# Hymba layer: first loads and norms reordered, P's diagonal blocks split between VectorE and ScalarE, another entry into the MLP

## The chip, the cores and the metric

The kernel runs on one core of one Trainium2 chip. The metric is the device time of one execution in microseconds (us). The engines are named as in the profile: PE (TensorE, matmuls and transposes), DVE (VectorE), ACT (ScalarE), POOL (GpSimd) and SP (SyncE, which here only starts DMAs). L12 is line 12 of the kernel's file.

## What is computed

One layer of a hybrid decoder in fp32: 1024 tokens of width 1024 with 16 meta tokens ahead of them (dropped at the end). One input projection feeds two token mixers, a retention with 4 heads and a sparse attention with 8 heads over the 256 best keys of each query; their outputs go through one output projection, and a squared-ReLU MLP of width 4096 follows.

```python
u = rmsnorm(h, norm1_w); proj = u @ w_in
rq, rk, rv, rg, dq, dk, dv, iq, ik, iw = split(proj)
y_ret = retention(rq, rk, rv, rg, ret_norm_w, pos)
# sparse attention, by blocks of 128 queries
score = einsum('bch,bchs->bcs', iw, relu(einsum('bchd,bsd->bchs', iq, ik)))
_, sel = top_k(where(causal, score, NEG), 256)
logits = q @ k[sel] + rel_bias[t5_bucket(dist)]
y_dsa = softmax(where(valid, logits, NEG)) @ v[sel]
h = h + concat([y_ret, y_dsa]) @ w_out
u = rmsnorm(h, norm2_w)
h = h + square(relu(u @ w_ff1)) @ w_ff2
```

## The kernel before, in words

**Products.** Every fp32 matrix is split into a rounded half `hi` and a rest `lo`; a product is three matmuls (hi·hi, hi·lo, lo·hi) into one PSUM bank. The hi half is an ACT copy, the lo half a subtraction on DVE or POOL. PSUM has two rings of banks, `psA` and `psB`.

**Order.** The program is written as Python generators that are woven together (`spread`), and a scheduler then places the instructions of each engine by its own estimate of their readiness, so the order on an engine isn't the order of the text. Each engine runs its own list in order. SP starts nearly all DMAs, in its list's order.

**First stage (0 to about 190 us).** For each block `b` of 128 tokens `do_norm1` (L250) loads `xt` (`load_x`, L177), and `norm_T` (L145) squares it on ACT with the row sum (L149), takes the inverse root on POOL (`rsqrt`, rs_y, L141 and L142), multiplies by it and by the norm's weight row `nrow` on DVE (L151, tile `u`), transposes `u` on PE (L156, eight 128x128) and splits the result (uh, ul). `small_proj` makes the index keys from `u` (weights `wrs`, halves `wsh`/`wsl`, L327 and L328), `index_q` and `index` the index scores (weights of the columns IQ: raws `wr`, L214; halves `wh`/`wl`, L189 and L194). The relative bias is looked up by one matmul with a one-hot table (`hot`, `relt`, L371 to L382): its result `gt` goes to DRAM as `g1`, and is spread there to 128 rows as `gd` (1.47 MB), from which `bias` is read at L438.

**Top-k, retention and attention (about 100 to 600 us).** DVE and ACT find the 256th best score of each query; PE meanwhile does the retention and the projections. Attention runs over eight blocks `i` and two head groups `g`: `attend_p` (L568) makes the logits and their exponentials P, `attend_v` (L607) transposes P on PE (L628), splits it into `ph` halves (ACT L633, DVE L634) and multiplies with the values (L635, L636). The first 16 keys (the meta tokens) of four heads go together: one transpose (L616), a copy `phm` on ACT (L618), and four DVE operations of 32 partitions each (L621) that put the hi rows (`odd` 0) and lo rows (`odd` 1) of each head into its own diagonal block of `pm`; a matmul with `pm` (L638) ends the group. There are 16 groups.

**Output projection and second norm (about 597 to 680 us).** `out_mm` (L689) makes the second half of the columns, block by block; the second half of `w_out` is loaded and split by `out_w(1, True)` when the first of nine pieces is done. `norm2` (L876) of each block follows: Square and row sum on ACT (L879), inverse root on POOL, product `un` on DVE (L881), eight transposes (L889). From these come the operands of the MLP's first layer, a Strassen-like scheme with seven products m = 2, 4, 3, 5, 6, 7, 1, each with its own sums of token halves: U2 and U4 from the blocks 0 to 3; U3, U5, U6 and U7 from the blocks 4 to 7 together with the kept copies `f1` of the first; U1 likewise in the MLP's loop (L1172, L1173). The lo halves (L895) of U4, U3 and U6 are made by POOL, the others by DVE.

**MLP (about 667 us to the end).** 16 column groups `p` with seven products each, one `unit` of 12 matmuls for each product (L1002 to L1004). The units' order is `groups`: products 2 and 4 of p = 1, all of p = 0, the rest of p = 1, then p = 2 and on, so four units need only U2 and U4. `EVAC` says how each product is added into four accumulators (1a, 1b, 2a, 2b): an ACT copy (L1009) where it is the first, a DVE addition (L1012) where not. The second layer follows (`stage2`, L1101, matmuls L1120 to L1122).

Of the kernel before, what the change touches and what calls it, by code (L numbers as in the profile page):

```python
# [81 lines left out]
def layer(ctx, tc, x, meta, norm1_w, w_in, ret_w, q_w, k_w, rel, w_out, norm2_w, w1, w2,  # L82
# [94 lines left out]
    def load_x(b):  # L177
        xt = xin.get(b)
        if xt is None:
            xt = row("xt")  # L180
        nc.sync.dma_start(xt[:, :D], x[128 * b:128 * b + 128, :])
        return xt
# [67 lines left out]
    def do_norm1(b):  # L250
        if b == 8:
            xm = row("xt")
            nc.sync.dma_start(xm[:NM, :D], meta)
            norm_T(xm[:NM, :D], NM, lambda g: (um[:, 4 * g:4 * g + 4, :NM], um[:, 4 * g:4 * g + 4, ML:]))
        else:
            o = 128 * (b % 4)
            xt = load_x(b)
# [111 lines left out]
    L = hot_d.shape[1]
    hot = wp.tile([32, L], F32, tag="rl", name="hot", bufs=2)  # L370
    nc.sync.dma_start(hot, hot_d)  # L371
    relt = const.tile([32, 8], F32, name="relt")
    nc.sync.dma_start(relt, rel)
    g1 = dr.tile([8, L], F32, name="g1")
    gd = dr.tile([128, 8, L], F32, name="gd")
    ps = psA()
    nc.tensor.matmul(ps[:8, :L], relt, hot, start=True, stop=True)
    gt = wp.tile([8, L], F32, tag="rl", name="gt", bufs=2)
    nc.scalar.activation(gt, ps[:8, :L], AF.Copy)
    nc.sync.dma_start(g1, gt)  # L380
    g1a = g1[:]
    nc.sync.dma_start(gd, bass.AP(tensor=g1a.tensor, offset=g1a.offset, ap=[[0, 128], [L, 8], [1, L]]))  # L382
# [839 lines left out]
```

## Time and profile before

| | us |
|---|---|
| median of three runs | 1297.18 |
| the three runs | 1294.48, 1297.18, 1297.89 |
| the profiled execution | 1296.34 |
| its span in the trace | 1294.6 |
| PE busy | 1240.1 (96%) |
| DVE busy | 1022.2 (79%) |
| ACT busy | 757.9 (59%) |
| POOL busy | 221.1 (17%) |

Of the profiled execution 1.7 us lie outside the span. All times in the text are of this one execution, from the span's start. Busy times are shares of the whole span; how an engine stands in one stage is read from the views of a stretch. A matmul's duration in the trace overlaps the next one's, so what a matmul costs PE is read from the distance of two starts.

### The profile page before, as it was taken

The numbers are of one execution on the slowest core, as the hardware profiler recorded it, in microseconds if no ns is written. First come the engines' busy times: TensorE is split into PE (matmuls) and PEld (weight loads), VectorE is DVE, ScalarE is ACT, GpSimd is POOL, SyncE is SP. The second block draws the span as 40 slices with busy tenths as digits, with TensorE's granted clock in tenths as the row PEclk, the third lists the DMA queues.
The fourth block names the chain that finished last, engine by engine and source line by source line (L and its number), as shares of the span: only waits on it lengthen the run. The fifth ranks groups of instructions, "written<-read, shape, count | busy, mean of one in ns | idle before, by whom it ended". The sixth has DMA issues, their size and how long they took to land.

```text
span 1294.6 us, 18365 instructions
## 1 busy us (share of the span) xinstructions
PE 1240.1 (96%) x6032; PEld 1025.8 (79%) x6032; DVE 1022.2 (79%) x2298; ACT 757.9 (59%) x1612; POOL 221.1 (17%) x278
## 2 busy tenths in 40 slices
PE   5999989999999899999898999999999999999998
PEld 4888868887887667877776888888888888888887
DVE  5579999993478899876489777777788887887875
ACT  6567567889956677665356555454565444444442
POOL 4003262424425322101241000000000200000000
PEclk8999999999999999999998999999999999999999
DMA  8103031202113223114953444344539835344222
GB/s 282 60 17 93 25 114 40 73 9 74 58 33 97 91 84 105 69 63 145 321 189 116 149 173 145 130 153 151 176 134 355 341 114 187 122 163 166 91 94 98
DMA packets 101279, 165.06 MB, mean 128 GB/s; under 512 B 8712, under 2 KB 48944, under 8 KB 97472
## 3 DMA queue, kind: packets, MB, share of 16 engines
q1 hardware_dynamic: 101184, 163.90, 36.7%
q8 instruction: 47, 0.77, 0.2%
q14 instruction: 48, 0.39, 0.1%
HBM read 113.46 MB, written 51.85 MB: 128 GB/s over the span
## 4 chain that ended last, share of the span: by engine, by line
PE 69%; DVE 19%; ACT 5%; issue 4%; DMA 2%; POOL 1%; SPq 0%; DVEq 0%; ACTq 0%
PE psB L1120 5%; PE psB L1121 5%; PE psB L1122 5%; PE psB L1002 4%; PE psB L1003 4%; PE psB L1004 4%; PE psA L1003 4%; PE psA L1002 4%; PE psA L1004 4%; DVE jk_cnt L746 3%; PE psA L246 3%; PE psA L247 3%; PE psA L248 3%; PE psA L1120 3%; PE psA L1121 3%
## 5 line engine op out<-in xcount | busy, mean ns | idle before, releaser
L973 ACT ACTIVATE wh<-ga 128x512 fp32r<-128x512 f32 x144 | 87.2, 628 | 159.2 <-PE psB L1121 138.3
L246 PE MATMUL psA<-wh,uh 128*128 128x512 f32 x376 | 150.3, 400 | 1.3 <-DVE fg L488 1.3
L247 PE MATMUL psA<-wh,ul 128*128 128x512 f32 x376 | 149.3, 397 | 0.0
L248 PE MATMUL psA<-wl,uh 128*128 128x512 f32 x376 | 149.1, 397 | 0.0
L974 DVE TENSOR_TENSOR wl<-ga,wh 128x512 fp32r<-128x512 f32 x144 | 96.6, 687 | 47.8 <-ACT wh L973 47.2
L973 ACT ACTIVATE wh<-sum 128x512 fp32r<-128x512 f32 x128 | 78.7, 625 | 79.2 <-DVE sum L970 70.9
L1121 PE MATMUL psB<-wh,wl 128*128 128x512 f32 x280 | 108.9, 389 | 0.0
L1122 PE MATMUL psB<-wl,wh 128*128 128x512 f32 x280 | 108.9, 389 | 0.0
L751 ACT ACTIVATE jk_top<-sc,tcand 128x784 bf16<-128x784 f32 (+2 forms) x93 | 98.3, 1057 | 14.9 <-DVE tcand L821 12.5
L1120 PE MATMUL psB<-wh 128*128 128x512 f32 x280 | 106.8, 389 | 0.0
L974 DVE TENSOR_TENSOR wl<-sum,wh 128x512 fp32r<-128x512 f32 x128 | 88.5, 693 | 4.0 <-ACT wh L973 4.0
L246 PEld LDWEIGHTS psA<-wh,uh 128*128 128x128 f32 x376 | 70.8, 188 | 14.0 <-issue 1.1
L248 PEld LDWEIGHTS psA<-wl,uh 128*128 128x128 f32 x376 | 70.8, 188 | 13.3
L247 PEld LDWEIGHTS psA<-wh,ul 128*128 128x128 f32 x376 | 71.1, 189 | 12.2
L1040 POOL COPY ga<-wl 128x1 f32<-128x1 f32 x8 | 6.6, 828 | 402.6 <-DVE wl L974 359.2
L746 DVE TENSOR_SCALAR_CACHE_REDUCE jk_cnt<-sc,tcand 128x400 bf16<-128x400 f32 (+2 forms) x93 | 70.4, 757 | 1.0
L359 ACT ACTIVATE rl<-psB,absw 128x320 f32<-128x320 f32 (+5 forms) x104 | 52.9, 555 | 28.0 <-DVE sc L363 13.9
L1121 PE MATMUL psA<-wh,wl 128*128 128x512 f32 x168 | 65.4, 389 | 0.0
L1122 PE MATMUL psA<-wl,wh 128*128 128x512 f32 x168 | 65.4, 389 | 0.0
L1120 PE MATMUL psA<-wh 128*128 128x512 f32 x168 | 64.9, 389 | 0.0
L194 POOL TENSOR_TENSOR wl<-wr,wh 128x512 fp32r<-128x512 f32 x44 | 60.3, 1390 | 19.2 <-ACT wh L189 13.9
L633 ACT ACTIVATE ph<-psB 128x512 fp32r<-128x512 f32 x72 | 41.4, 594 | 34.9 <-PE psB L628 26.8
(391 smaller groups left out, 3559.0 us busy)
## 6 DMA issues: line engine op xcount, KB each, us to landing
ga<-hid SPq DMA_DIRECT2D x28, 1024.0 KB, 5.2
wr<-in_w_ff_dram SPq DMA_DIRECT2D x34, 512.0 KB, 5.1
hid<-hs SPq DMA_DIRECT2D x48, 256.0 KB, 2.1
wr<-in_w_in_dram SPq DMA_DIRECT2D x32, 256.0 KB, 3.2
ysd<-ys SPq DMA_DIRECT2D x32, 256.0 KB, 2.8
ys<-ysd SPq DMA_DIRECT2D x32, 256.0 KB, 5.0
gb<-in_w_ff_dram SPq DMA_DIRECT2D x8, 1024.0 KB, 6.8
ga<-in_w_ff_dram SPq DMA_DIRECT2D x8, 1024.0 KB, 5.2
```

The costliest lines, as they stand in the source:

```text
L246: nc.tensor.matmul(ps[:P, :n], uh, wh, start=d == 0, stop=False)
L247: nc.tensor.matmul(ps[:P, :n], ul, wh, start=False, stop=False)
L248: nc.tensor.matmul(ps[:P, :n], uh, wl, start=False, stop=d == 7)
L746: nc.vector.tensor_scalar(jk_[:, :ncol[i]], sc[i], cand[:, j:j + 1], 0.0, op0=ALU.is_ge, op1=ALU.add, accum_out=cnt[:, j:j + 1])
L973: nc.scalar.activation(view(hi), s, AF.Copy)
L974: nc.vector.tensor_tensor(view(lo), s, view(hi).bitcast(F32), op=SUB)
L1002: nc.tensor.matmul(ps, hi[:, a], uh[:, d], start=d == 0, stop=False)
L1003: nc.tensor.matmul(ps, lo[:, a], uh[:, d], start=False, stop=False)
L1004: nc.tensor.matmul(ps, hi[:, a], ul[:, d], start=False, stop=d == 3)
L1120: nc.tensor.matmul(ps[tb], ah[:, t], bh, start=j == 0 and m not in CONT, stop=False, skip_group_check=True)
L1121: nc.tensor.matmul(ps[tb], al[:, t], bh, start=False, stop=False, skip_group_check=True)
L1122: nc.tensor.matmul(ps[tb], ah[:, t], bl, start=False, stop=j == NO - 1, skip_group_check=True)
```

## The change

It has three parts.

**First stage.** The load of block 0 is SP's first DMA, ahead of `ident` and `nrow`. `norm_T` scales `xt` in place (ACT's Square writes its unused output to a scratch tile instead of `u`). The loads of block 1, the meta tokens and blocks 2 and 3 are written right behind the small weights, later blocks' two rounds ahead of their norm. The one-hot matmul and its DMAs move from the top into `far_bias`, called behind the index scores of block 2. The IQ weights are loaded within the round of block 0.

**P's diagonal blocks.** One DVE operation on 128 partitions (L630) takes the place of the four on 32; its output lies beside `phm`. Four ACT copies of 32 partitions (L633) put its pieces into `pm`.

**Entry into the MLP.** All lo halves of `norm2` are made by DVE. The halves of U7 and U1 are made in the MLP's loop (`late_halves`, at units 5, 6 and 7, 8), from `f1`, whose second half now also takes its sum; a four-element POOL copy ahead of each keeps them behind U3. `groups` has six units that need only U2 and U4 (products 2 and 4 of p = 1, p = 2 and p = 0). `EVAC` copies each of the first three products once, and DVE makes the other accumulators from them. The raws of the second half of `w_out` are written ahead of the loop, their splits together with the next piece; the first MLP weights are loaded one piece earlier, and their first two operands are made within the loop.

```diff
+    xin = {0: row("xt")}
+    nc.sync.dma_start(xin[0], x[0:128, :])
     ident = const.tile([128, 128], F32, name="ident")
...
-        nc.scalar.activation(u[:P, :D], src, AF.Square, scale=D ** -0.5, accum_out=ss[:P])
+        nc.scalar.activation(jk_top[:P, :D], u, AF.Square, scale=D ** -0.5, accum_out=ss[:P])
         r = rsqrt(ss[:P], 1, 1.0, P)
-        nc.vector.scalar_tensor_tensor(u[:P, :D], src, r[:P], nrow[:P], op0=ALU.mult, op1=ALU.mult)
+        nc.vector.scalar_tensor_tensor(u, u, r[:P], nrow[:P], op0=ALU.mult, op1=ALU.mult)
...
+    def far_bias():
+        hot = wp.tile([32, L], F32, tag="rl", name="hot", bufs=2)
+        nc.sync.dma_start(hot, hot_d)
...
+        nc.sync.dma_start(gd, bass.AP(tensor=g1a.tensor, offset=g1a.offset, ap=[[0, 128], [L, 8], [1, L]]))
+        return gd
     do_norm1(0)
...
-    ih, il = load_cols(w_in, [(IQ, 512)], alt=True)
+    for b in (1, 8, 2):
+        load_x(b)
+    for b in (1, 8):
+        do_norm1(b)
+    load_x(3)
     for b in range(NB):
         if b + 2 < NB:
+            if b + 4 < NB:
+                load_x(b + 4)
             do_norm1(b + 2)
...
+            ih, il = load_cols(w_in, [(IQ, 512)], alt=True)
         if b:
             index(b, index_q(b))
+        if b == 2:
+            gd = far_bias()
...
-        hi = small.tile([128, 128], F32R, name="phm", tag="ytmp", bufs=1)
-        nc.scalar.activation(hi, tp[:, :128], AF.Copy)
+        hi = small.tile([128, 2, 128], F32R, name="phm", tag="ytmp", bufs=1)
+        nc.scalar.activation(hi[:, 0], tp[:, :128], AF.Copy)
+        nc.vector.scalar_tensor_tensor(hi[:, 1], tp[:, :128], odd, hi[:, 0].bitcast(F32), op0=ALU.mult, op1=ALU.subtract)
         for hh in range(4):
             z = slice(32 * hh, 32 * hh + 32)
-            nc.vector.scalar_tensor_tensor(pm[z, hh], tp[z, :128], odd[z], hi[z].bitcast(F32),
-                                           op0=ALU.mult, op1=ALU.subtract)
+            nc.scalar.activation(pm[z, hh], hi[z, 1].bitcast(F32), AF.Copy)
...
-        def halves(m, x, eng):
+        def halves(m, x):
             h, l = [v[:, :, s] for v in U[m]]
             nc.scalar.activation(h, x, AF.Copy)
-            eng.tensor_tensor(l, x, h.bitcast(F32), op=SUB)
+            nc.vector.tensor_tensor(l, x, h.bitcast(F32), op=SUB)
...
+    def late_halves(m, tb):
+
+        s = slice(128 * tb, 128 * tb + 128)
+        h, l = [v[:, :, s] for v in U[m]]
+        x = f1[m == 7][:, tb]
+        nc.scalar.activation(h, x, AF.Copy)
+        nc.vector.tensor_tensor(l, x, h.bitcast(F32), op=SUB)
...
-    EVAC = {2: [("1b", 1), ("2b", -1)], 4: [("1b", "+"), ("1a", 1)], 3: [("2a", 1), ("2b", "+")], 5: [("2a", "+"), ("1a", "-")],
+
+    EVAC = {2: [("1b", "=")], 4: [("1a", "=")], 3: [("2a", "="), ("2b", "1b"), ("1b", "1a")], 5: [("2a", "+"), ("1a", "-")],
...
-    groups = [(1, ORD[:2]), (0, ORD), (1, ORD[2:])] + [(p, ORD) for p in range(2, NP)]
+    groups = [(1, ORD[:2]), (2, ORD[:2]), (0, ORD), (1, ORD[2:]), (2, ORD[2:])] + [(p, ORD) for p in range(3, NP)]
...
+        for m, n0 in ((7, 5), (1, 7)):
+            if n == n0:
+                nc.gpsimd.tensor_copy(U[m][0][:, 0, 0:512:128], U[3][1][:, 0, 384:388].bitcast(F32))
+            for tb in (2 * (n - n0), 2 * (n - n0) + 1):
+                if 0 <= tb < 4:
+                    late_halves(m, tb)
```

At the program's start, POOL before has the inverse roots (rs_y) of block 0, block 1 and the meta tokens, then two lo halves of the IQ weights, then the root of block 2:

```order
L141 TENSOR_TENSOR rs_y<-ss,eps_91 16x1
L142 TENSOR_TENSOR rs_y<-rs_y,nhalf 16x1
L194 TENSOR_TENSOR wl<-wr,wh 128x512 x2
L141 TENSOR_TENSOR rs_y<-ss,eps_91 128x1
L142 TENSOR_TENSOR rs_y<-rs_y,nhalf 128x1
```

In the changed kernel the same place on POOL reads:

```order
L143 TENSOR_TENSOR rs_y<-ss,eps_93 16x1
L144 TENSOR_TENSOR rs_y<-rs_y,nhalf 16x1
L143 TENSOR_TENSOR rs_y<-ss,eps_93 128x1
L144 TENSOR_TENSOR rs_y<-rs_y,nhalf 128x1
L143 TENSOR_TENSOR rs_y<-ss,eps_93 128x1
L144 TENSOR_TENSOR rs_y<-rs_y,nhalf 128x1
L328 TENSOR_TENSOR wsl<-wrs,wsh 128x200
L196 TENSOR_TENSOR wl<-wr,wh 128x512
```

The roots of blocks 2 and 3 have moved ahead of the first lo half of the IQ weights.

On ACT, in the attention of one of the later blocks, the changed kernel has the four copies into `pm` (L633) once with three other instructions between them and the `phm` copy (L629) that starts the group:

```order
L629 ACTIVATE phm<-psB 128x128
L689 ACTIVATE ys<-yd 128x512
L576 ACTIVATE qs<-psA 64x4x128
L607 ACTIVATE P,sums<-P,m_6365 128x784
L644 ACTIVATE ph<-psB 128x512
L625 ACTIVATE rx<-rs 128x256
L633 ACTIVATE pm<-phm 32x128 x4
```

and a little later, on the same engine, with none:

```order
L607 ACTIVATE P,sums<-P,m_6519 128x912
L629 ACTIVATE phm<-psB 128x128
L633 ACTIVATE pm<-phm 32x128 x4
L644 ACTIVATE ph<-psB 128x512
L607 ACTIVATE P,sums<-P,m_6563 128x912
```

The second form, in which ACT has nothing to do between `phm` and DVE's operation on it, stands in 6 of the 16 groups; in the others two to five instructions lie between. Before, ACT's list has only the `phm` copy there and DVE's the four operations.

At the end of the second norm, DVE before comes from the last block's residual sum (`hrow`, L702) to its product `un` (L881) by these rows:

```order
L702 TENSOR_TENSOR hrow<-psB,hp 128x512
L974 TENSOR_TENSOR wl<-sum,wh 128x512 x2
L902 TENSOR_TENSOR ut<-ut,psB 128x512
L902 TENSOR_TENSOR ut<-psB,f_7118 128x512
L895 TENSOR_TENSOR u7l<-ut,u7h 128x4x128
L970 TENSOR_TENSOR sum<-wr_7811 128x512
L970 TENSOR_TENSOR sum<-wr_7799,wr_7811 128x512
L881 SCALAR_TENSOR_TENSOR un<-hrow,rs_y,nrow_2080 128x1024
```

and now by these, with the product of the block ahead of it among them:

```order
L713 TENSOR_TENSOR hrow<-psB,hp 128x512
L920 TENSOR_TENSOR ut<-ut,psB 128x512
L906 TENSOR_TENSOR u6l<-ut,u6h 128x4x128
L892 SCALAR_TENSOR_TENSOR un<-hrow,rs_y,nrow_2071 128x1024
L993 TENSOR_TENSOR wl<-sum,wh 128x512
L993 TENSOR_TENSOR wl<-wr_7853,wh 128x512
L993 TENSOR_TENSOR wl<-wr_7841,wh 128x512
L993 TENSOR_TENSOR wl<-sum,wh 128x512
L906 TENSOR_TENSOR u3l<-ut,u3h 128x4x128
L989 TENSOR_TENSOR sum<-wr_7841 128x512
L892 SCALAR_TENSOR_TENSOR un<-hrow,rs_y,nrow_2071 128x1024
```

Two of the lo halves there (u6l, u3l) stood on POOL, and u7l is gone from the place. On PE 23 matmuls of products 2 and 4 stand between the last two blocks' transposes, and 24 of product 2 between the last transposes and the first matmul of product 3; before it was 13 and 12.

## Rows read from the trace of the kernel before

**Rows 1.** Page, part 1: busy time, share of the span, instructions.

```profile
PE 1240.1 (96%) x6032; PEld 1025.8 (79%) x6032; DVE 1022.2 (79%) x2298; ACT 757.9 (59%) x1612; POOL 221.1 (17%) x278
```

**Rows 2.** Busy time of each engine in stretches; PEclk is the granted clock.

```profile
0.00:40.00 40.00, 25.98 (x149) 22.50 (x150) 21.47 (x52) 24.51 (x63) 16.48 (x31) 0.91 0.77 244
24.00:28.00 4.00, 3.68 (x19) 3.59 (x20) 3.19 (x12) 3.51 (x9) 1.28 (x1) 0.50 0.97 379
400.00:600.00 200.00, 183.30 (x1042) 148.31 (x1041) 167.91 (x591) 137.28 (x344) 48.25 (x34) 0.99 0.26 88
440.00:560.00 120.00, 113.64 (x650) 92.77 (x650) 108.26 (x403) 86.35 (x203) 27.58 (x14) 1.00 0.24 83
600.00:640.00 40.00, 36.35 (x164) 28.73 (x163) 20.53 (x28) 14.49 (x26) 7.43 (x9) 0.96 0.83 283
666.00:700.00 34.00, 26.39 (x108) 20.65 (x107) 34.00 (x50) 23.43 (x42) 12.71 (x9) 0.85 0.34 110
700.00:1294.00 594.00, 590.94 (x2608) 488.97 (x2606) 472.47 (x758) 282.93 (x503) 9.29 (x18) 1.00 0.45 162
```

**Rows 3.** Waits of PE in the whole span: total us, times, longest us.

```profile
PE psA L377 <- DMA relt<-in_rel_bias_dram: 7.8, 1, 7.8
PE psB L156 <- DVE u L151: 6.0, 2, 4.2
...
PE psB L1002 <- ACT u3h L894: 2.9, 1, 2.9
...
PE psB L889 <- DVE un L881: 1.9, 1, 1.9
```

**Rows 4.** Timeline of the start: start us, duration us, engine, operation, [idle <-releaser].

```profile
1.65 0.43 SPq L181 DMA_DIRECT2D xt<-in_x_dram  x1
7.21 1.06 ACT L149 ACTIVATE u<-xt 128x1024 f32<-128x1024 f32 x1 [5.19 <-DMA xt<-in_x_dram]
7.78 1.38 PE L377 MATMUL psA<-hot,relt 32*8 32x367 f32 x2 [7.78 <-DMA relt<-in_rel_bias_dram]
9.29 1.62 DVE L151 SCALAR_TENSOR_TENSOR u<-xt,rs_y,nrow 128x1024 f32<-128x1024 f32 x1
10.97 1.97 PE L156 MATMUL psB<-ident,u 128*128 128x128 f32 x8 [1.81 <-DVE u L151]
17.83 4.25 POOL L194 TENSOR_TENSOR wl<-wr,wh 128x512 fp32r<-128x512 f32 x2 [0.62 <-ACT wh L189]
24.32 1.94 PE L156 MATMUL psB<-ident,u 128*128 128x128 f32 x8 [4.17 <-DVE u L151]
```

**Rows 5.** Attention: DVE and ACT in time, line L621, ACT's 128x64 copies by form.

```profile
481.83 0.27 ACT L618 ACTIVATE phm<-psB 128x128 fp32r<-128x128 f32 x1
483.63 1.43 DVE L621 SCALAR_TENSOR_TENSOR pm<-psB,kss,phm 32x128 fp32r<-32x128 f32 x4
L621 DVE SCALAR_TENSOR_TENSOR pm<-psB,kss,phm x64: 329/346/364, 419.1 to 595.3; 32x128 fp32r<-32x128 f32 x64
L517 DVE SCALAR_TENSOR_TENSOR oh<-psB,rs_y,fg x32: 333/343/352, 232.0 to 423.4; 128x128 f32<-128x128 f32 x32
L599 ACT ACTIVATE few<-P 128x64 f32<-128x64 f32 x32 | 7.6, 250 | 2.0 <-PE psB L616 1.8
```

**Rows 6.** Entry into the MLP in time, and line L881 (ns min/median/max).

```profile
L881 DVE SCALAR_TENSOR_TENSOR un<-hrow,rs_y,nrow x8: 1285/2301/2337, 625.4 to 675.9; 128x1024 f32<-128x1024 f32 x8
674.28 2.80 POOL L895 TENSOR_TENSOR u3l<-ut,u3h 128x512 fp32r<-128x512 f32 x1 [0.32 <-ACT u3h L894]
675.86 2.30 DVE L881 SCALAR_TENSOR_TENSOR un<-hrow,rs_y,nrow 128x1024 f32<-128x1024 f32 x1
678.09 0.68 DVE L895 TENSOR_TENSOR u5l<-psB,u5h 128x512 fp32r<-128x512 f32 x1
...
683.07 0.63 PE L1003 MATMUL psB<-u2h,wl 128*128 128x512 f32 x1
683.50 0.63 PE L1004 MATMUL psB<-u2l,wh 128*128 128x512 f32 x1
```

More of the change, by code (lines that the diff above doesn't have):

```diff
@@ L177, in load_x @@
     def load_x(b):
[L178 to L182, printed above, removed]
+        if b not in xin:
+            xin[b] = row("xt")
+        if b == 8:
+            nc.sync.dma_start(xin[b][:NM, :D], meta)
+        elif b:
+            nc.sync.dma_start(xin[b][:, :D], x[128 * b:128 * b + 128, :])
     altc = [0]
@@ L250, in do_norm1 @@
     def do_norm1(b):
+        xt = xin.pop(b)
         if b == 8:
[L252 to L254 removed]
+            norm_T(xt[:NM, :D], NM, lambda g: (um[:, 4 * g:4 * g + 4, :NM], um[:, 4 * g:4 * g + 4, ML:]))
         else:
             o = 128 * (b % 4)
[L257 removed]
             norm_T(xt[:, :D], 128, lambda g: (uth[b // 4][g][:, :, o:o + 128], utl[b // 4][g][:, :, o:o + 128]))
@@ L366, in index @@
                                 base=0, channel_multiplier=1)
-    do_norm1(0)
[L369 to L382, printed above, removed]
-    sh, sl = load_small()
-    do_norm1(1)
-    do_norm1(8)
-    ih, il = load_cols(w_in, [(IQ, 512)], alt=True)
+    L = hot_d.shape[1]
+    def far_bias():
+        hot = wp.tile([32, L], F32, tag="rl", name="hot", bufs=2)
+        nc.sync.dma_start(hot, hot_d)
+        relt = const.tile([32, 8], F32, name="relt")
+        nc.sync.dma_start(relt, rel)
+        g1 = dr.tile([8, L], F32, name="g1")
+        gd = dr.tile([128, 8, L], F32, name="gd")
+        ps = psA()
+        nc.tensor.matmul(ps[:8, :L], relt, hot, start=True, stop=True)
+        gt = wp.tile([8, L], F32, tag="rl", name="gt", bufs=2)
+        nc.scalar.activation(gt, ps[:8, :L], AF.Copy)
+        nc.sync.dma_start(g1, gt)
+        g1a = g1[:]
+        nc.sync.dma_start(gd, bass.AP(tensor=g1a.tensor, offset=g1a.offset, ap=[[0, 128], [L, 8], [1, L]]))
+        return gd
+    do_norm1(0)
+    sh, sl = load_small()
+    for b in (1, 8, 2):
[3 more added lines that the diff above has]
+    load_x(3)
     for b in range(NB):
         if b + 2 < NB:
+            if b + 4 < NB:
+                load_x(b + 4)
             do_norm1(b + 2)
@@ L1144, in layer, with w_out_raw, w_out_split @@
     pre = out_prep(*todo[0])
+    wraw = {}
+    def w_out_raw(g):
+        wraw[g] = wp.tile([128, 2, 512], F32, tag="wr", name="wr", bufs=3)
+        nc.sync.dma_start(wraw[g], w_out[256 * g:256 * g + 256, 512:].rearrange("(j p) w -> p j w", p=128))
+    def w_out_split(g):
+        for j in range(2):
+            d = 2 * g + j
+            for v, k in zip(split(wraw[g][:, j], 512, True, rgain[:, d:d + 1] if d < 4 else None), range(2)):
+                ow[0][k].append(v)
+    for g in range(3):
+        w_out_raw(g)
     for k, (ch, b) in enumerate(todo):
         if k == 1:
-            out_w(1, True)
-        nxt = out_prep(*todo[k + 1]) if k < NB else None
+            ow[0] = [], []
+            for g in range(4):
+                if g == 1:
+                    nxt = out_prep(*todo[k + 1])
+                    w_out_raw(3)
+                w_out_split(g)
+        else:
+            nxt = out_prep(*todo[k + 1]) if k < NB else None
         spread((8, out_mm(ch, b, *pre)), *([(1.3, norm_step(b - 1))] if k >= 2 else []))
@@ L1153, in layer @@
         pre = nxt
-        if k == 6:
+        if k == 5:
             w1_load(0, 0)
             w1_load(0, 1)
-    for n in range(2):
-        prep1(n)
+        if k in (6, 7):
+            prep1(k - 6)
     for _ in norm_step(7):
```

58 lines of the change are left out of this document (28 added, 30 removed).

## The prediction

> **What bounds the kernel now.** I read the busy times first [rows 1]: PE works 1240.1 of 1294.6 us, so nothing gains unless it takes idle time or slow clock away from PE, and at most some 54 us can be had. The busy times by stretch [rows 2] say where these lie. From 700 us to the end PE works 590.94 of 594 us, so the MLP behind its entry can give nothing. Three stretches are left that the change touches: the first 40 us (14.0 us idle, granted clock 0.91), the attention from 400 to 600 us (16.7 us idle), and the entry into the MLP from 666 to 700 us (7.6 us idle, granted clock 0.85). PE's waits [rows 3] name what ends last there: at the start a DMA and then DVE's product `u`, at the MLP's entry DVE's `un`, DVE's sums and ACT's halves of U3. In the attention the idle time is spread over many short waits, and DVE is the fullest engine beside PE: 108.26 of 120 us, 90%, between 440 and 560 us, ACT 86.35, 72% [rows 2].
>
> **First stage.** Block 0's data is there at 7.2 us, issued as SP's third DMA at 1.65; ACT's Square, POOL's root and DVE's product follow, and PE has its first transposes at 10.97 [rows 4]. The new order puts this load in front. Its data then comes earlier by at least the two issues that stood ahead of it, some 0.45 us each (its own shows 0.43). DVE's product also needs `nrow`, now the last of the same three transfers, so I let it arrive when block 0's data did, at 7.2. The product takes 1.62 us [rows 4], which puts the first transposes at 8.9: 2.0 us gained (0.9 to 2.1). The one-hot matmul leaves a place where PE had nothing else, since it waited 7.8 us for `relt` [rows 3] and then another 1.8 us for `u` [rows 4]; in its new place, in PE's running stream, it costs what it lasts, 1.38 us at most [rows 4]; I take half, 0.7, since a clock at its upper level would halve it (an estimate).
>
> The second gap at the start is 4.17 us of waiting for `u` of block 2, up to 24.32 [rows 4]. In POOL's queue the root for that product stood behind two lo halves of the IQ weights, 4.25 us from 17.83 on [rows 4]. The change has this root ahead of them, and block 2's load ahead of the IQ weights on SP, so the gap goes: 4.2 us. Behind the gap PE ran at the lower of its two clock levels, granted 0.50 from 24 to 28 us with 3.68 us of work [rows 2]; the same work at the full clock takes 1.8, so about 2 us more. What is late next are the IQ weights. They are now issued behind four more blocks of `x` (0.5 MB each) and ahead of the 1.47 MB of `gd`, which stood before them; the DMAs moved 244 GB/s in the first 40 us [rows 2], so 0.5 MB is 2.1 us, and between two blocks too late and none I put 2.5 us of the gain back. Sum: 2.0 + 4.2 + 2.0 - 0.7 - 2.5 = **5.0 us gained** (1 to 7.5). The DMAs that are moved behind (`hot`, `g1`, `gd`) hold SP while ACT makes `gt`, and block 7's load is queued behind them; its norm comes some rounds later, so I cost it at nothing, and at 2 us inside the range where that cover is gone.
>
> **P's diagonal blocks.** One of the 64 DVE operations lasts 346 ns, four in a row 1.43 us [rows 5]. A product of the same kind on 128 partitions lasts 343 ns (L517), so DVE sheds (1.43 - 0.35) x 16 groups = 17.3 us. ACT gets 64 copies of 32x128. The trace has no copy of 32 partitions; the nearest are 128x64 with 250 ns and 128x128 with 270 ns [rows 5], so 16.0 to 17.3 us for all; I take 17, since as on DVE the rows' length sets the time and not the partitions. ACT goes from 72% to some 80% in the middle, DVE from 90% to 80%. Half of PE's 6.4 us of idle time between 440 and 560 us [rows 2] is what I give back for that, and 0.8 us in the rest of the stretch, where DVE isn't so full: **4 us gained**. Bounds: no more than 9 (all 6.4 and a quarter of the other 10.3), and on the other side a loss of 3, because the way to `pm` now has one engine more: ACT, DVE, ACT, PE, with 0.35 + 1.1 us in it where DVE's 1.43 was.
>
> On DVE 32 partitions cost as much as 128, 346 ns against 343 [rows 5]. [...]
>
> **Entry into the MLP.** From 666 to 700 us DVE works 34.00 of 34 us [rows 2], so here it sets the pace. PE idles 7.6 us, and after its gaps it runs at the lower clock: starts 0.43 us apart [rows 6], where the MLP needs 0.23 for one (590.94 us for 2608 [rows 2]). Some 19 matmuls run so, 19 x 0.2 = 4.0 us. In all 11.6 us can be had. The change does three things to it. Twelve lo halves move from POOL to DVE, where one takes 0.68 us alone and 0.60 in a row: 7.2 us more. In exchange DVE is no longer slowed by POOL: `un` lasts 1.29 us alone and mostly 2.30 where POOL works beside it, as from 674.28 on [rows 6]; eight of them give back up to 7 us. And the eight lo halves of U7 and U1 leave the place for the MLP's loop, where PE is the bound and DVE has room (472.47 of 594 [rows 2]).
>
> I walk through DVE's new order with 0.60 us for a subtraction and 1.2 for `un`. It reaches the last residual sum at about 672 us, as now, the product of the last block but one ends at 674.5, that of the last at 679.4. PE, done with the output projection at 666.4, has 24 matmuls of product 4 (5.4 us) and is at the last but one's transposes at 671.9: it waits 2.7 us. Then 23 matmuls carry it to 680.7, past the last `un`, and 24 more to 687.0, when DVE and ACT have made the halves of U3 up to about a microsecond. With 2.7 and 1 us of gaps and about 1 us of slow clock behind, 4.7 us of the 11.6 stay: **7 us gained** (3 to 10). The two units pulled ahead, one ACT copy less for each p and the copies of `EVAC` made otherwise lie beside a PE with 3 us of idle time in 594, so they cost and gain nothing.
>
> **The rest.** The raws and halves of `w_out`'s second half come in another order. PE idles 3.7 us from 600 to 640 [rows 2]; I leave that as it is, with 2 us on either side.
>
> **The sum.** 5 + 4 + 7 = 16 us. The profiled execution took 1296.34 us, so 1280.3; the median of the runs is 0.8 above it: **1281 us**.
>
> **The rivals.** (a) **DVE stays the bound at the MLP's entry.** For it speaks 34.00 of 34 us busy; against it that POOL's work, which slows `un`, goes. If the lo halves cost more than they give back, the products come 7 us later, and the stage gains nothing: 1281 + 7 = 1288. (b) **The first stage keeps its gap**, for the IQ weights instead of `u`. For it: 2 MB of weights behind more of `x`; against it: as many bytes of `gd` are moved behind them. The 5 us are gone: 1286. Both at once: 1293. (c) **ACT is held in its own queue, slower.** In 6 of the 16 groups the copies into `pm` stand right behind `phm`, so ACT waits there for DVE's operation, and behind it stand the copies `ph` that PE's products need. In the one group shown DVE came to its operation at 483.63, 1.5 us after `phm` had ended at 482.10 [rows 5]. With 0.35 for the operation itself ACT would be held 1.9 us, over 16 groups 30 us. What of it reaches PE decides: from 12 / 16 = 0.75 us a group on, the 12 us won in the other stages are spent. At 1.2 us, 19 in all, and without the 4 us won there, it is 1281 + 4 + 19 = 1304. Against it: ACT idles 28% there, and in ten groups two to five instructions lie between. (d) **The change does little of what it says**, as the scheduler already had the order: true for `w_out`'s raws at most, since POOL's and ACT's lists differ as shown; it has no time of its own.
>
> **How the numbers follow.** Forecast 0.60; (a) 0.12; (b) 0.10; both, 0.09; (c) 0.09. Measured runs of this kernel can tell a difference from about 0.3%, 3.9 us. Forecast, (a) and (b) lie below 1293.3, so faster has 0.82; both at once is 0.09 for the same; (c) is 0.09 for slower. The range goes from all terms at their good ends, 1297 - 7.5 - 9 - 10 = 1271, to both at once, 1293; (c) is left out, and a part of the tails.
>
> **What would show it.** First stage: first transposes near 9 us, no wait for `u` of block 2, and the clock not halved near 25 us; wrong if PE waits there for a weight's halves. Diagonal blocks: DVE's busy time from 400 to 600 us less by 17 us, ACT's more by about as much, PE's waits for `pm` and `ph` shorter; wrong if ACT's wait for `phm` on DVE is over a microsecond each. MLP: `un` at 1.3 us, one gap of 2 to 3 us ahead of the last but one block's transposes, nothing over 1 us ahead of product 3; wrong if waits for DVE there still sum to over 7 us. The whole is wrong above all if the copies on ACT hold up `ph`.

## The result

| | us |
|---|---|
| before, median of 4 runs | 1296.28 (1294.48 to 1297.89) |
| changed, median of 4 runs | 1275.43 (1274.97 to 1277.10) |
| ratio, 95% interval | 0.9842 (0.9825 to 0.9859) |
| forecast | 1281, range 1271 to 1293 |
| changed, the profiled execution and its span | 1275.67, 1273.9 |

The kernel is faster by 20.9 us where 16 were forecast. Busy times after, whole span (part 1 of the page) and by stretch, with the columns of [rows 2]:

```profile
PE 1235.0 (97%) x6032; PEld 1024.1 (80%) x6032; DVE 1006.3 (79%) x2262; ACT 770.5 (60%) x1660; POOL 207.1 (16%) x268
...
0.00:40.00 40.00, 29.18 (x164) 25.54 (x165) 26.38 (x55) 26.45 (x67) 19.70 (x33) 0.91 0.70 225
24.00:28.00 4.00, 4.00 (x25) 3.92 (x25) 4.00 (x9) 2.01 (x6) 1.97 (x3) 0.58 0.20 76
400.00:600.00 200.00, 185.98 (x1057) 150.78 (x1055) 153.81 (x544) 158.71 (x407) 46.20 (x29) 0.99 0.26 92
...
600.00:640.00 40.00, 38.16 (x178) 30.69 (x177) 21.03 (x31) 17.72 (x33) 7.13 (x12) 1.00 0.96 340
666.00:700.00 34.00, 33.84 (x154) 27.78 (x152) 33.29 (x56) 23.39 (x43) 1.07 (x4) 1.00 0.32 108
700.00:1270.00 570.00, 570.00 (x2516) 471.85 (x2514) 461.15 (x742) 271.29 (x477) 8.62 (x18) 1.00 0.47 168
```

The MLP's entry, 26.39 of 34 us busy before [rows 2], is now 33.84, at the full clock (granted 1.00, before 0.85). In the attention DVE has shed 14.1 us and ACT taken 21.4, and PE's busy time has moved by 2.7 only.

Where the time went is seen best at matmuls that both kernels run in the same order. The first and last start of a line is in the view of one line; here are four of PE, first of before, then of the changed kernel (one retention product, the product that ends each attention group, the output projection, the MLP's second layer):

```profile
L500 PE MATMUL psB<-qkT x64: 270/275/377, 203.3 to 416.8; 128*128 128x128 f32 x64
L638 PE MATMUL psB<-pm,vv x16: 389/398/792, 421.8 to 606.2; 128*128 128x512 f32 x16
L694 PE MATMUL psB<-wh,ys x128: 387/389/628, 439.2 to 665.6; 128*128 128x512 f32 x128
L1120 PE MATMUL psB<-wh x280: 389/389/389, 987.5 to 1290.1; 128*128 128x512 f32 x140
```

```profile
L511 PE MATMUL psB<-qkT x64: 270/275/580, 199.9 to 413.5; 128*128 128x128 f32 x64
L649 PE MATMUL psB<-pm,vv x16: 387/396/499, 418.8 to 601.2; 128*128 128x512 f32 x16
L705 PE MATMUL psB<-wh,ys x128: 389/389/504, 436.5 to 657.9; 128*128 128x512 f32 x128
L1144 PE MATMUL psB<-wh x280: 389/389/389, 966.8 to 1269.4; 128*128 128x512 f32 x140
```

The changed kernel is 3.4 us ahead at the first retention product, 3.3 at its last (413.5 against 416.8), 5.0 at the attention's end, 7.7 at the output projection's end and 20.7 from the second layer on, to the last matmul. Matching every matmul by its line and order, and taking the median lead of those that started in 20 us, gives 3.2 at 100 to 400 us, 5.0 at 600, 8.6 at 640 and 20.7 from 680 on; "lead" below is this number, and a loss is a difference of two leads.

| stretch | forecast | lead gained |
|---|---|---|
| first stage | 5 (1 to 7.5) | 3.2 |
| attention | 4 (-3 to 9) | 1.8 |
| output projection | 0 (-2 to 2) | 3.6 |
| entry into the MLP | 7 (3 to 10) | 12.1 |

So the forecast was right in its sign and within its range, and its terms were not. Two of them came 4.0 us short and two 8.7 us over, so that the sum is only 5 us off is in part luck.

### The profile page after: what moved, and what is told of

It reads as the page before. It is cut to its first block, busy times and chain, and to the rows that moved or that the text cites. A ratio compares the mean times of both kernels' runs of the same rounds, so it can differ in the third digit from the quotient of the medians.

```text
span 1273.9 us, 18372 instructions
## 1 busy us (share of the span) xinstructions
PE 1235.0 (97%) x6032; PEld 1024.1 (80%) x6032; DVE 1006.3 (79%) x2262; ACT 770.5 (60%) x1660; POOL 207.1 (16%) x268
## 4 chain that ended last, share of the span: by engine, by line
PE 75%; DVE 13%; ACT 5%; DMA 3%; issue 3%; POOL 0%; SPq 0%; ACTq 0%; DVEq 0%
PE psB L1145 5%; PE psB L1144 5%; PE psB L1146 5%; PE psA L248 4%; PE psA L249 4%; PE psA L250 4%; PE psA L1023 4%; PE psA L1021 4%; PE psA L1022 4%; PE psB L1023 4%; PE psB L1021 4%; PE psB L1022 4%; PE psA L1145 3%; PE psA L1144 3%; PE psA L1146 3%
## 5 line engine op out<-in xcount | busy, mean ns | idle before, releaser
L645 DVE TENSOR_TENSOR ph<-psB,ph 128x512 fp32r<-128x512 f32 x72 | 48.6, 687 | 18.9 <-ACT ph L644 16.3
```

## The experiments

All are timed beside the kernel before on the same chip. Each edit is to the changed kernel (1275.4 us), except for one that says otherwise.

### The entry into the MLP

**m_pool**: the lo halves of U4, U3 and U6 on POOL again.

```diff
-        def halves(m, x):
+        def halves(m, x, eng=nc.vector):
...
-            halves(4, t)
+            halves(4, t, nc.gpsimd)
...
-            halves(3, t)
+            halves(3, t, nc.gpsimd)
...
-            halves(6, t)
+            halves(6, t, nc.gpsimd)
```

> The changed kernel (1275.4 us), with the lo halves of U4, U3 and U6 on POOL again. Traces before and after: at the same matmul PE is 8.7 us earlier at 666 us and 20.7 us earlier from 700 us on, so the MLP's entry gave 12.1 us where I forecast 7. Theory A, POOL beside DVE was what made the entry slow (un 2.30 us, now 1.28 in all eight): un goes back to about 2.3 us, DVE falls behind by some 1 us for each of the later blocks, PE waits 3 us or more in all between 640 and 700 us: 1280 to 1285 us. Theory B, the two units pulled ahead and the late halves of U7 and U1 made it: DVE is slower but PE has cover, within 2 us of 1275.4.

**m_four**: four units ahead of product 3.

```diff
-    groups = [(1, ORD[:2]), (2, ORD[:2]), (0, ORD), (1, ORD[2:]), (2, ORD[2:])] + [(p, ORD) for p in range(3, NP)]
+    groups = [(1, ORD[:2]), (0, ORD), (1, ORD[2:])] + [(p, ORD) for p in range(2, NP)]
...
-        for m, n0 in ((7, 5), (1, 7)):
+        for m, n0 in ((7, 3), (1, 5)):
```

> The changed kernel with four units ahead of product 3 instead of six, as before (the late halves two units earlier as well). The trace after shows one wait of 0.2 us at product 3, so the cover is nearly used up there: 24 matmuls of 0.23 us, 5.4 us, are taken out ahead of it. Theory B (the order of the units made the entry's gain): PE waits about 5 us for the halves of U3 and U6 and has some 2 us of slow clock behind it: 1280 to 1283 us. Theory A (POOL's lo halves alone were the cause): DVE is in time anyway, within 2 us of 1275.4.

**b_dve**: the kernel before with these lo halves on DVE, nothing else.

```diff
-            total(4, tps[1], g1, SUB, nc.gpsimd)
+            total(4, tps[1], g1, SUB, nc.vector)
...
-            total(3, t, tps[1], SUB, nc.gpsimd)
+            total(3, t, tps[1], SUB, nc.vector)
...
-            total(6, tps[0], g1, ADD, nc.gpsimd)
+            total(6, tps[0], g1, ADD, nc.vector)
```

> The kernel before (1296.3 us) with one edit, the lo halves of U4, U3 and U6 on DVE instead of POOL. Theory A: un goes from 2.3 to 1.3 us, DVE's other operations beside POOL to 0.68, and DVE loses no more than it gains; PE's 11.6 us of loss at the entry shrink by 3 to 6 us: 1290 to 1293 us. Theory B: DVE is busy 34.00 of 34 us there, so 7.2 us of lo halves come late without another order of units: 1296 to 1301 us, no gain.

**m_early**: the halves of U7 within norm2 and those of U1 at units 3 to 6.

```diff
             halves(6, t)
+            halves(7, g2)
...
-        for m, n0 in ((7, 5), (1, 7)):
-            if n == n0:
-                nc.gpsimd.tensor_copy(U[m][0][:, 0, 0:512:128], U[3][1][:, 0, 384:388].bitcast(F32))
-            for tb in (2 * (n - n0), 2 * (n - n0) + 1):
-                if 0 <= tb < 4:
-                    late_halves(m, tb)
+        if 3 <= n < 7:
+            late_halves(1, n - 3)
```

> The changed kernel with the halves of U7 made within norm2 and those of U1 at units 3 to 6, as before; six units and lo halves on DVE stay. With the earlier runs the entry's 12.1 us split into 7.3 for the two units pulled ahead and 4.5 for POOL's lo halves, and the lo halves alone gave the kernel before nothing. If the late halves carry a share of their own (four copies and four lo halves, 2.4 us of DVE and 2.4 of ACT, fall between the blocks' sums again): PE waits 2 to 5 us more for the halves of U3 or U6, 1278 to 1281 us. If the cover of six units is enough without them: within 1.5 us of 1275.4.

| | median us | ratio to before | loss at the entry, us (of lead, from 640 to 680) |
|---|---|---|---|
| m_pool | 1279.2 (1278.7 to 1279.6) | 0.9864 (0.9848 to 0.9881) | 3.9 |
| m_four | 1282.1 (1280.7 to 1284.2) | 0.9889 (0.9873 to 0.9906) | 7.3 |
| m_early | 1279.4 (1277.5 to 1281.2) | 0.9873 (0.9858 to 0.9887) | 4.0 |
| b_dve | 1298.2 (1295.7 to 1300.9) | 1.0010 (0.9999 to 1.0020) | 1.3 (against before) |

PE's waits tell where each loses: total us, times, longest, from 590 to 720 us, in m_pool, then m_four, m_early and b_dve; the last block is one line of the kernel before that [rows 3] leave out.

```profile
PE psB L1023 <- POOL u3l L906: 1.7, 1, 1.7
...
PE psB L900 <- DVE un L892: 0.5, 1, 0.5
PE psB L1021 <- ACT u3h L905: 0.5, 1, 0.5
```

```profile
PE psB L1021 <- ACT u3h L905: 3.2, 1, 3.2
```

```profile
PE psB L1024 <- DVE u3l L906: 2.5, 1, 2.5
```

```profile
PE psB L1002 <- ACT u3h L894: 4.1, 1, 4.1
PE psB L1002 <- DVE ut L902: 3.6, 1, 3.6
...
PE psB L889 <- DVE un L881: 0.3, 1, 0.3
```

```profile
PE psB L1002 <- DVE ut L902: 1.6, 1, 1.6
```

And the line of the product `un` in the changed kernel, in m_pool and in b_dve (ns min/median/max):

```profile
L892 DVE SCALAR_TENSOR_TENSOR un<-hrow,rs_y,nrow x8: 1276/1280/1285, 620.8 to 666.8; 128x1024 f32<-128x1024 f32 x8
```

```profile
L892 DVE SCALAR_TENSOR_TENSOR un<-hrow,rs_y,nrow x8: 1274/1280/2308, 620.2 to 667.6; 128x1024 f32<-128x1024 f32 x8
```

```profile
L881 DVE SCALAR_TENSOR_TENSOR un<-hrow,rs_y,nrow x8: 1278/1281/1287, 626.6 to 673.6; 128x1024 f32<-128x1024 f32 x8
```

What follows: no one part makes the entry. In b_dve, with the lo halves off POOL, `un` takes 1.28 us in all eight, where five of eight took 2.30 before, and yet b_dve gains nothing. DVE's own extra work comes there, 7.2 us for twelve lo halves at 0.60 (an estimate, from their starts in a row), and while PE's wait for `un` falls from 1.9 [rows 3] to 0.3 us, its two long waits grow from 2.9 [rows 3] and 1.6 us to 4.1 and 3.6.

In m_pool `un` is slow in only three of eight, and what PE waits for is POOL's own lo half of U3, which takes DVE 0.68 us:

```profile
L906 POOL TENSOR_TENSOR u3l<-ut,u3h x4: 1368/2177/2796, 651.3 to 677.4; 128x512 fp32r<-128x512 f32 x4
```

So theory A of m_pool had the size nearly right (1279.2 us, just under its range) and the way wrong. The units pulled ahead are the largest share, as theory B of m_four had it; POOL's lo halves and the early halves of U7 and U1 each cost about 4 us when they are put back. Taken back one at a time the three sum to 15.2 us, more than the 12.1 of the whole: they aren't a sum, each is worth its price only beside the others. Where each is taken back, the granted clock from 666 to 700 us is lower again, 0.95 in m_pool, 0.90 in m_four, 0.95 in m_early, after 1.00 in the changed kernel; in m_four 512-column matmuls start 0.43 us apart behind the 3.2 us of waiting, up to 683.4 us, and 0.23 after that. The new order of `EVAC` and the earlier load of the first MLP weights weren't undone by themselves.

### The output projection

**o_wout**: the second half of w_out as before.

```diff
-    for g in range(3):
-        w_out_raw(g)
     for k, (ch, b) in enumerate(todo):
         if k == 1:
-            ow[0] = [], []
-            for g in range(4):
-                if g == 1:
-                    nxt = out_prep(*todo[k + 1])
-                    w_out_raw(3)
-                w_out_split(g)
-        else:
-            nxt = out_prep(*todo[k + 1]) if k < NB else None
+            out_w(1, True)
+        nxt = out_prep(*todo[k + 1]) if k < NB else None
```

> The changed kernel with the second half of the output weights loaded and split as before, at once in the loop's second round. PE gained 3.6 us between 600 and 640 us (5.0 us earlier at 600, 8.6 at 640), where I had forecast none. Theory A, the weights' raws and splits written apart made it: the wait for wh of 1.5 us and the slow clock behind the waits (2 us) come back, 1278 to 1280 us. Theory B, the gain comes with the earlier and other order of the attention's end: within 1.5 us of 1275.4.

Measured: 1275.9 us (1275.2 to 1280.5), ratio 0.9848 (0.9826 to 0.9869), so no difference that these runs can show. Its trace loses 2.0 us of lead between 600 and 640, where PE waits again (from 590 to 720 us):

```profile
PE psB L706 <- DMA ys<-ysd: 2.0, 1, 2.0
PE psB L705 <- ACT wh L191: 1.1, 1, 1.1
```

It had won 1.8 us ahead of that, where the changed kernel's trace has a stretch at the lower clock level, 413.1 to 416.5 us (granted 0.50), that this one has not (granted 1.00 from 400 to 600 us). The traces of s_third and s_bias, whose edits lie in the first stage, lack that stretch too (granted 1.00 from 400 to 600 us in both), so a lead read from one trace is good to some 2 us only. By these traces, then, 2.0 of the 3.6 us of the output projection are the new way to load and split these weights; the other 1.6 are about as much as the half clock of before from 625.8 to 629.2 us cost (granted 0.50; eight matmuls start 0.43 us apart instead of 0.23, so 1.6 us, an estimate), which neither trace has any more (1.00 from 600 to 640 us in both).

### P's diagonal blocks

**p_four**: four DVE operations of 32 partitions again.

```diff
...
-        nc.vector.scalar_tensor_tensor(hi[:, 1], tp[:, :128], odd, hi[:, 0].bitcast(F32), op0=ALU.mult, op1=ALU.subtract)
...
-            nc.scalar.activation(pm[z, hh], hi[z, 1].bitcast(F32), AF.Copy)
+            nc.vector.scalar_tensor_tensor(pm[z, hh], tp[z, :128], odd[z], hi[z].bitcast(F32),
+                                           op0=ALU.mult, op1=ALU.subtract)
```

> The changed kernel with P's diagonal blocks made by four DVE operations of 32 partitions, as before. From 400 to 600 us the change gained 1.8 us where I forecast 4; DVE's busy time there fell by 14.1 us and ACT's rose by 21.4. Theory A, DVE's relief is what gained it and is small, since PE waits for many things in turn: 1276.5 to 1278.5 us. Theory B, ACT's 64 copies (307 ns each, 19.6 us) cost what DVE's relief gave, and the 1.8 us come from the order alone: within 1 us of 1275.4, or faster.

**p_nocopy**: without the copies, so `pm` keeps its zeros and the meta tokens' share of these products is left out of the result.

```diff
-        for hh in range(4):
-            z = slice(32 * hh, 32 * hh + 32)
-            nc.scalar.activation(pm[z, hh], hi[z, 1].bitcast(F32), AF.Copy)
```

> The changed kernel without the four ACT copies into pm: P's products with the meta tokens' values are left out of the result in effect (pm keeps its zeros), so this is the price of the copies alone. Theory A (PE waits in turn for many things, ACT has room): within 1 us of 1275.4. Theory B (the copies cost what DVE's relief gave): 2 to 4 us less, 1271 to 1273.5 us, with the waits of PE for ph on ACT, 3.6 us in the changed kernel, down to 1 us.

**p_pool**: the copies on POOL.

```diff
-            nc.scalar.activation(pm[z, hh], hi[z, 1].bitcast(F32), AF.Copy)
+            nc.gpsimd.tensor_copy(pm[z, hh], hi[z, 1].bitcast(F32))
```

> The changed kernel with the four copies into pm on POOL instead of ACT. POOL is busy 46 of 200 us there, ACT 159. A POOL copy of this size isn't in the trace; its 128x512 subtraction takes 1.28 us and its 128x1 operations 0.2 to 0.55, so I take 0.4 to 0.6 us each. Theory B (ACT's copies cost): 1 to 3 us less, 1272.5 to 1274.5. Theory A: no gain, and the group's path to pm is longer by up to 1 us, of which PE sees little: 1275 to 1278.

| | median us | ratio to before | DVE, ACT, POOL busy, 400 to 600 us |
|---|---|---|---|
| p_four | 1280.0 (1277.5 to 1282.6) | 0.9877 (0.9862 to 0.9893) | 167.6, 137.7, 46.1 |
| changed | 1275.4 (1275.0 to 1277.1) | 0.9842 (0.9825 to 0.9859) | 153.8, 158.7, 46.2 |
| p_pool | 1279.4 (1277.0 to 1281.2) | 0.9875 (0.9858 to 0.9892) | 151.2, 137.9, 64.2 |
| p_nocopy | 1269.6 (1269.1 to 1271.6) | 0.9800 (0.9785 to 0.9814) | 158.6, 143.4, 48.1 |

The line of the copies, in the changed kernel on ACT, and in p_pool on POOL:

```profile
L633 ACT ACTIVATE pm<-phm x64: 289/307/311, 417.5 to 590.6; 32x128 fp32r<-32x128 f32 x64
its engine sat idle before it (us, times) until:
  DVE phm L630: 3.3, 6
```

```profile
L633 POOL CAST pm<-phm x64: 281/288/296, 416.4 to 593.4; 32x128 fp32r<-32x128 f32 x64
```

And PE's waits for `pm`, `phm` and ACT's `ph` from 400 to 600 us, before, then in the changed kernel, p_four and p_nocopy:

```profile
PE psB L638 <- DVE pm L621: 2.1, 3, 0.9
PE psB L616 <- DVE pm L621: 1.0, 2, 0.5
PE psB L635 <- ACT ph L633: 1.0, 3, 0.5
...
PE psB L628 <- DVE pm L621: 0.5, 2, 0.3
```

```profile
PE psB L646 <- ACT ph L644: 3.6, 5, 1.5
...
PE psB L639 <- DVE phm L630: 0.5, 1, 0.5
```

```profile
PE psB L646 <- ACT ph L644: 3.1, 5, 1.3
```

```profile
PE psB L643 <- ACT ph L641: 1.8, 4, 0.8
```

The copies cost 5.9 us by the medians of p_nocopy and the changed kernel, more than theory B had. DVE's relief alone is therefore worth more than the change kept of it; p_four loses 4.5 us by the medians, more than either of its theories had. Its trace loses 3.8, most of it where it runs at the half clock from 420.1 to 427.0 us (granted 0.97 from 400 to 600 us, 0.99 in the changed kernel), so how much of it is DVE and how much the clock behind it, the trace doesn't separate. On POOL the copies take no longer, 288 ns, and the kernel loses 4.0 us by the medians, again outside of both ranges. Its trace loses 2.2: PE waits for other things (`ys` and `few`, made by ACT, 1.7 and 1.0 us in the wait view), and it has one stretch of 3.4 us at the lower clock level more (granted 0.98 from 400 to 600 us). Why the move costs more than it frees on ACT stayed open.

What it is about the copies that costs isn't shown. p_nocopy takes away their time on ACT and the longer way to `pm` at once, and PE's wait for ACT's `ph` is nearly as long in p_four, where ACT has no such copies. p_pool, which frees ACT and keeps the way, gains nothing.

**p_vvt**: no copies, same result. The operation on `phm` is the moving operand itself, and the zeros go into the stationary one, which never changes.

```diff
-        nc.sync.dma_start(vv[NM * a:NM * a + NM, 8].bitcast(F32), vm2[:NM, a % 2].bitcast(F32))
+        nc.sync.dma_start(pm[NM * a:NM * a + NM, a // 2].bitcast(F32), vm2[:NM, a % 2].bitcast(F32))
...
-            nc.scalar.activation(pm[z, hh], hi[z, 1].bitcast(F32), AF.Copy)
...
-                nc.tensor.matmul(pv, vv[:, 8], pm.rearrange("p h n -> p (h n)"), start=False, stop=True)
+                for hh in range(4):
+                    nc.tensor.matmul(pv[:, 128 * hh:128 * hh + 128], pm[:, hh], hi[:, 1], start=False, stop=hh == 3)
```

> The changed kernel without the copies into pm, with the same result: the meta tokens' values stand once, before the attention, as four block-diagonal stationary tiles, and each group ends in four matmuls of 128 columns (one for each head, straight from DVE's operation on phm) instead of one of 512 columns. Leaving the copies out had given 6.5 us. PE pays for it: a 128-column matmul takes 0.11 us or a little more where 512 columns take 0.23, so 0.2 to 0.3 us a group, 3.3 to 5 us for 16. Theory B (ACT's copies stand in PE's way and cost about 7 us): 1271.5 to 1274, faster than the changed kernel by 2 to 4 us. Theory A (PE waits in turn for many things): 1276 to 1279, slower by PE's extra work.

Measured: 1276.7 us (1274.3 to 1279.7), ratio 0.9851 (0.9827 to 0.9875): inside theory A's range, but not for its reason. Its trace wins 8.8 us of lead between 380 and 600 us and has lost 9.8 before: from 200 to 380 us the scheduler wove another order, it seems because `pm`'s DMAs had moved behind later loads. PE there:

```profile
238.99 0.77 PE L248 MATMUL psA<-wh,uh 128*128 128x512 f32 x1 [2.62 <-DVE fg L499]
239.55 0.63 PE L249 MATMUL psA<-wh,ul 128*128 128x512 f32 x1
239.98 0.63 PE L250 MATMUL psA<-wl,uh 128*128 128x512 f32 x1
...
300.61 0.79 PE L518 MATMUL psB<-vz,sm 128*128 128x128 f32 x2 [1.55 <-DVE sm L515]
```

Behind each of these waits 512-column matmuls start 0.43 us apart, not 0.23: the clock stood at its lower level from 238.0 to 244.9 and from 299.5 to 306.3 us.

**p_vd**: the same, with the tile cleared and filled early, where `vv`'s column was.

```diff
-    vv = kp_.tile([128, 9, 128], F32R, name="vv")
+    vv = kp_.tile([128, 8, 128], F32R, name="vv")
+    pm = kp_.tile([128, 4, 128], F32R, name="pm")
+    nc.gpsimd.memset(pm.bitcast(F32), 0.0)
```

> The block-diagonal stationary tiles once more, cleared at the program's start and filled by the same early DMAs as the column of vv that they replace, so that every engine's order ahead of the attention is the changed kernel's. In the earlier form those DMAs came late, the scheduler wove retention and projection otherwise, and PE lost 9.8 us against the changed kernel between 200 and 380 us (waits of 2.6 us and 1.6 us, and two stretches of 6.8 us at the lower clock level, 238.0 to 244.9 and 299.5 to 306.3), which the attention gave back. Theory B (ACT's copies cost about 7 us, PE's extra 128-column matmuls little): 1266.5 to 1270 us. Theory A (what the attention gave back was only the delay): 1274 to 1277.

Measured: **1271.4 us** (1269.5 to 1273.2, 5 runs), ratio 0.9805 (0.9787 to 0.9824): faster than the changed kernel by 4.0 us, between the ranges of the two theories. The loss from 200 to 380 us is gone with the late DMAs: its lead there moves by 0.7 us only. It has a stretch at the lower clock level from 424.9 to 431.7 us that the changed kernel has not (granted 0.97 from 400 to 600 us, there 0.99); at 0.43 us instead of 0.23 for a matmul that is about 3 us (an estimate), more than the 1.4 us that it lacks to theory B's 1270. PE at one group's end in the changed kernel, then in p_vvt, whose group ends in the same way as p_vd's:

```profile
601.18 0.39 PE L649 MATMUL psB<-pm,vv 128*128 128x512 f32 x1
601.41 0.63 PE L705 MATMUL psB<-wh,ys 128*128 128x512 f32 x2
```

```profile
451.56 0.56 PE L647 MATMUL psB<-phm,pm 128*128 128x128 f32 x4
451.95 0.35 PE L598 MATMUL psA<-knh,qs 128*128 128x288 f32 x1
```

By the distance of starts four matmuls of 128 columns took 0.39 us, the median of p_vd's 16 groups too, where 512 columns took 0.23: 0.16 us in each of 16 groups, 2.6 us of PE's time, for 64 copies off ACT.

### The first stage

**s_third**: block 0's load behind `ident` and `nrow`.

```diff
     xin = {0: row("xt")}
-    nc.sync.dma_start(xin[0], x[0:128, :])
     ident = const.tile([128, 128], F32, name="ident")
...
     nc.sync.dma_start(nrow, bcast(norm1_w, D))
+    nc.sync.dma_start(xin[0], x[0:128, :])
```

> The changed kernel with block 0's load behind those of ident and nrow again. The changed start gained 3.2 us by 100 us, where I forecast 5; PE's first transposes stand at 8.22 us instead of 10.97, and DVE's product waited 2.0 us for nrow. Theory A, the early load made most of it: first transposes at 9.5 to 10 us and 1 to 2 us lost for good, 1276.5 to 1277.5. Theory B, the order of the roots and loads made it, and an earlier first block only waits later (for the halves of block 1 and the small weights): the lead is gone by 30 us, within 0.7 us of 1275.4.

**s_bias**: the relative bias at the top.

```diff
     do_norm1(0)
+    gd = far_bias()
     sh, sl = load_small()
...
-        if b == 2:
-            gd = far_bias()
```

> The changed kernel with the relative bias' matmul and its DMAs right behind block 0's norm again. Theory A, the late bias carries a share of the start's 3.2 us because the 1.47 MB of gd no longer stand ahead of the weights: 1 to 2.5 us lost, 1276.5 to 1278. Theory B, the bias fits in the DMAs' idle time there and its matmul in PE's: within 0.7 us of 1275.4.

s_third: 1275.5 us (1274.8 to 1279.3), ratio 0.9846 (0.9824 to 0.9868). s_bias: 1274.8 us (1273.9 to 1275.1), ratio 0.9834 (0.9813 to 0.9854). Neither differs from the changed kernel, theory B for both by the times. By the traces, the late load costs 0.4 us of lead at 100 us, though PE's first wait grew by 2.7 us (8.2 to 10.9), and the early bias 1.2 us, which its trace has back by 420 us. The rest of the 3.2 us, some 1.6 us, is left for the roots and loads of blocks 1 to 3 ahead of the weights; that part wasn't undone by itself.

## Why the prediction was right, and where its terms were not

**First stage, 5 forecast, 3.2 measured.** PE's first waits and DVE's product in the changed kernel, from its timeline:

```profile
6.88 1.28 DVE L152 SCALAR_TENSOR_TENSOR xt<-xt,rs_y,nrow 128x1024 f32<-128x1024 f32 x1 [2.00 <-DMA nrow<-in_norm_w_dram]
8.22 1.97 PE L157 MATMUL psB<-ident,xt 128*128 128x128 f32 x8 [8.22 <-DVE xt L152]
...
20.72 1.12 PE L157 MATMUL psB<-ident,xt 128*128 128x128 f32 x4 [0.99 <-DVE ul L160]
22.53 0.40 PE L237 MATMUL psA<-wsh,um 128*48 128x200 f32 x1 [0.70 <-DVE um L160]
```

The step on `nrow` held: it lands last and sets the product, at 6.88 instead of 7.2, and the product took 1.28 us, so the first transposes came 2.75 us earlier rather than 2.0. But s_third shows that only 0.4 of it stay. In its trace PE has 0.8 us of waits behind the first transposes, in the changed kernel 2.6, and both come to their faster pace at the same time: 200-column matmuls start 0.17 to 0.21 us apart up to 27.4 us in the changed kernel, but for a few around 19 us, and up to 27.0 in s_third, and about 0.11 apart behind that. The gap of 4.17 us [rows 4] went as forecast, and in its place stand shorter ones, 2.1 us in four waits between 18 and 23 us. The clock's 2 us weren't had: from 24 to 28 us it was granted 0.58, after 0.50 [rows 2], behind these four waits. The IQ weights' 2.5 us weren't lost either: PE waits for none of them. Three terms were off, and they nearly cancelled.

**Diagonal blocks, 4 forecast.** The lead says 1.8, the undoing 4.5 us by the medians. Half of the mechanism was as told: DVE less by 14.1 us (17.3 forecast), PE's waits for `pm`, 3.6 us in three lines of the wait view of before, down to 0.5 us on `phm`. Mis-sized was ACT's term: 307 ns for a copy (289 to 311), where I took 250 to 270 from the nearest rows. Quartering the partitions saved nothing on ACT either: 307 ns for 32 of them, against 270 for the `phm` copy of 128 out of PSUM [rows 5]. 64 of them are 19.6 us, and they cost PE 5.9 us (p_nocopy). That ACT was near enough to the path for this I had not seen; 72% busy over a stretch said too little. My own sign of being wrong, copies that hold up `ph`, showed in part: PE's waits for ACT's `ph` grew from 1.0 to 3.6 us, in five places, though to 3.1 in p_four too.

**Entry into the MLP, 7 forecast, 12.1 measured.** The step that failed is the walk's first number. I let DVE reach the last residual sum at 672 us "as now" and went on from there. In the timelines of DVE, before and then in the changed kernel:

```profile
663.50 2.34 DVE L881 SCALAR_TENSOR_TENSOR un<-hrow,rs_y,nrow 128x1024 f32<-128x1024 f32 x1
...
671.05 0.68 DVE L702 TENSOR_TENSOR hrow<-psB,hp 128x512 f32<-128x512 f32 x1
```

```profile
659.40 0.68 DVE L713 TENSOR_TENSOR hrow<-psB,hp 128x512 f32<-128x512 f32 x1
...
661.20 1.28 DVE L892 SCALAR_TENSOR_TENSOR un<-hrow,rs_y,nrow 128x1024 f32<-128x1024 f32 x1
...
666.80 1.28 DVE L892 SCALAR_TENSOR_TENSOR un<-hrow,rs_y,nrow 128x1024 f32<-128x1024 f32 x1 [0.71 <-POOL rs_y L144]
```

The sum runs at 659.40, 1.5 us behind the last output matmul's start (657.9), where before it was 5.5 (665.6), and DVE even waits 0.71 us for a root. POOL's slowing of DVE is the smaller part of that: the distance is 4.4 us in b_dve, where POOL is out of the way, and 2.5 in m_pool, where it is back. The larger part is the order. Before, the last sum stood behind the product `un` of the block ahead and seven more operations, from 663.50 to 671.05; in the new list, which I had before me, it stands ahead of that product. In m_pool, m_four and m_early it stands there too, so which edit moved it stayed open. A walk through a new list has to start ahead of the first operation that has changed its place. PE's 2.7 us of waiting and the slow clock behind it then fell away (granted 1.00 from 666 to 700 us), and 0.2 us is all that is left at U3's halves. The price of POOL was also read too high: five of the eight `un` were slow before (about 2.30 us against 1.28), so they could give back about 5 us and not up to 7.

**The rest, 0 forecast, 3.6 measured.** I had left PE's idle 3.7 us there as they were. By the traces about half of the gain was the weights' order (2.0 us, o_wout), and the other half is about what the half clock behind the waits cost before (1.6 us, an estimate).

**The rivals.** (a) was wrong for this kernel but is what b_dve does: with the lo halves alone nothing is gained. (b) and (c) were wrong: no wait for IQ weights, and ACT was held for `pm` 3.3 us in 6 groups, at most 0.9 each, not 1.9; but the copies themselves, which (c) counted for nothing, took the larger part of what DVE's relief gave, 5.9 of 10.4 us (p_four against p_nocopy).

## What to carry to other kernels

Cover in front of a late operand is one chain: a change to the engines that make it can show nothing alone (b_dve) and be worth 4 us beside the work put on PE ahead of it (m_pool); so undo parts of the whole, don't only add them one at a time. When a busy engine's order is followed by hand, read the new list from the first place where it differs, and take over no time from the old trace behind that. A block-diagonal operand can go on the side of a matmul that doesn't change: built once, it took 64 copies out of the loop here for 2.6 us of PE.

## What the runs showed of the hardware

A copy of 32 partitions by 128 elements took about the same on either engine, 307 ns on ACT in the changed kernel and 288 on POOL in p_pool (medians), and on ACT more than a 128x64 one (250 ns, [rows 5]). Four matmuls of 128 columns took 0.39 us together in p_vvt, 1.7 times the 0.23 of one of 512. A subtraction of 128x512 on POOL took 1.28 us at its fastest in the kernel before and up to 2.80 while DVE worked [rows 6], and DVE's product of 128x1024 1.28 and up to 2.34. And behind some waits PE lost more than the wait: in p_vvt, behind one of 2.6 us, the clock stood at its lower level up to 244.9 us, 6.9 us in all, and with 0.43 us instead of 0.23 for each of some 13 matmuls of 512 columns about 2.6 us more were lost than the wait view shows (an estimate).
